# First gate/up phase: w_down sums and block combinations on GpSimd, with their stores on GpSimd's queue

## The chip, the cores and the metric

The kernel runs on one core of a Trainium2 chip. A core has TensorE (matrix products into PSUM, PE in the profile), VectorE (DVE), ScalarE (ACT), GpSimd (POOL) and SyncE (SP), which only issues transfers. Each engine works through its own instructions strictly in order; semaphores hold an instruction back until what it needs is there. A transfer (DMA) is issued by an instruction in the queue of SP, ACT or GpSimd and then runs by itself. The metric is the device time of one execution in microseconds, as the median of several runs.

## The reference

The kernel computes one decoder layer over 2048 tokens of width 1024 in float32. What is behind the change is its feed-forward part:

```python
hn = rms_norm(h, ffn_pre_g)
ff = (jax.nn.silu(hn @ w_gate) * (hn @ w_up)) @ w_down      # 1024 -> 2816 -> 1024
h = h + rms_norm(ff, ffn_post_g)
```

Before it come an input projection, sliding-window attention, a causal convolution of width 31 over 512 channels (its 31 multiplications and additions per position are called taps) and an output projection.

## The kernel before, in words

Every product of two float32 matrices is made of three passes of a reduced format (`F32R`): each operand is split into a high part (ACT copies it, line 782 for the weights of this stage) and a low part (the rest, a subtraction on DVE or GpSimd, line 786 or, where DVE's helper records it, line 85), and high-high, high-low and low-high are added up in PSUM (line 108 is the matmul of all stages).

The tokens are taken in four tiles of 512. The feed-forward part works on two tiles at once, and there are two rounds: tiles 0 and 1 (names end in F for the gate/up phase and G for the down projection; in the code `ws[0]` is 0), then tiles 2 and 3 (`ws[0]` is 2). Inside a round, the two halves of the tokens and the two halves of the features make 2 x 2 blocks, and a scheme of seven block products instead of eight is used. For gate and up (`stage_p1`), the weight blocks A11 to A22 of a pair of 128-column groups give sums S1 to S4 (on DVE, `chl@F`), the activations' sums T1 to T4 are made once. A pair of column groups is worked for the gate and then for up; each takes five steps of 12 matmuls where two of the seven products were made earlier (`stage_pre`; their partial sums are kept in DRAM as `keeps` and loaded back into `gb`), and seven where not (the last of the 11 pairs).

The outputs of a pair are four blocks: the gate's goes through Silu on ACT into a tile `fa` (line 1038), the up product is multiplied onto it on DVE. `fa` has four buffers, so ACT can write a pair's outputs only when the stores of the pair before have read the same buffers. The down projection (`stage_p2`) is again the scheme of seven products; its operands are the four blocks and their sums, and the seven kinds are stored in DRAM as `mids`. Line 1045 stores a block as it is (two of a pair, and three in the last pair; in the other ten the third was stored by `stage_pre` and is loaded back by line 1014); then four combinations are made in place (lines 1050 and 1053), each overwriting a block, and stored (lines 1051 and 1054). A combination that overwrites a block that is being stored waits until that store has landed. In both rounds these later stores are put off by two steps (`defer`) and bound to the matmul of that time (`tied`), and they are issued by SP. In round one the combinations run on DVE (`vtt`), in round two on GpSimd (`ptt`).

The same scheme needs sums of w_down's blocks. `stage_tsums` makes them once, beside the first gate/up phase: for each of 11 pairs four blocks are loaded (line 1072, into `wx`, one buffer of two halves, and two of the three buffers of `fc`), four subtractions are made on DVE (`wx@G`, `fc@G`), and each result is stored as `td` (line 1078) by SP. A pair's buffers can be loaded again when its stores have landed.

Beside the main line run lanes, generators that are advanced by a fixed rate per step: the convolution's taps on DVE (`fc@C`), the sums of w_down, the output projection of later tiles. All this only gives the order in which instructions are emitted. A scheduler then fixes the order on each engine, by its own estimate of when each can run, and assigns buffers; the chip runs that order.

SP issues nearly all loads: raw weights (lines 956 and 958), the kept partial sums (line 988), w_down (1072). A store in its queue whose operand isn't ready holds up the loads behind it.

Of the kernel before, what the change touches and what calls it, by code (L numbers as in the profile page):

```python
# [18 lines left out]
ALU = mybir.AluOpType  # L19
# [18 lines left out]
def layer_kernel(ctx, tc, x, xT, cols, rows, sinks, relb, onehot, w_in, w_pw, w_out, w_gate, w_up, w_down, out):  # L38
    nc = tc.nc
# [15 lines left out]
    def t_(tag, shape, dt=F32):  # L55
        return sb.tile(list(shape), dt, tag=tag, name=nm(tag), bufs=BUFS[tag])

    def f4(tag, shape=(P, D)):
        return t_(tag, shape)

    def f2(tag, shape=(P, T)):
        return t_(tag, shape)

    def hl(tag):
        return t_(tag, (P, 2, T), F32R)
# [17 lines left out]
    def dve(op):  # L83
        def emit(*args, **kw):
            r = op(*args, **kw)  # L85
            if not paced[0]:
                pace["main"] = r.ins
            elif pace["main"] is not None and pace["main"] is not pace["tied"]:
                tc.add_manual_dep(
                    r.ins,  # L90
                    pace["main"].name,
                    mybir.DependencyInfo(mybir.DependencyClass.NoSync, mybir.DependencyReason.DATA),
                    reason="conv taps keep pace with the projections",
                )
                pace["tied"] = pace["main"]
            return r

        return emit

    stt = dve(nc.vector.scalar_tensor_tensor)  # L100
    vtt = dve(nc.vector.tensor_tensor)
    vts = dve(nc.vector.tensor_scalar)
    ptt = nc.gpsimd.tensor_tensor
# [9 lines left out]
    def tied(r):  # L113
        if lead_pe[0] is not None and lead_pe[0] is not r:
            after_first(lead_pe[0], r)
        return r
# [3 lines left out]
    def defer(n, emit):  # L120
        later.append([n, emit])

    def run_later():
        for item in later:
            item[0] -= 1
        while later and later[0][0] <= 0:
            later.pop(0)[1]()
# [52 lines left out]
    def after_first(first, r):  # L180
        tc.add_manual_dep(
            r.ins,
            first.ins.name,
            mybir.DependencyInfo(mybir.DependencyClass.NoSync, mybir.DependencyReason.DATA),
            reason="order",
        )
# [594 lines left out]
    def split_f(x, w):  # L781
        act(w[:, 0], x, AF.Copy)  # L782
        return w

    def lo(x, w, on_pool):
        (ptt if on_pool else vtt)(w[:, 1], x, w[:, 0].bitcast(F32), ALU.subtract)
# [155 lines left out]
    def stage_p1(ws, ops, mid, keep):  # L942
        PRE = PRES[ws[0]]
        L = f"F{ws[0]}"
        raws = {}
        todo = []
        for m in range(len(MATS)):
            st = [1, 2, 4, 5, 6] if m < PRE else list(range(7))
            todo += [(m, j, i, len(st)) for j, i in enumerate(st)]

        def loads(m):
            if m < len(MATS):
                lab[0] = L
                src, pr = MATS[m]
                r0 = t_("raw", (P, 2, T))
                nc.sync.dma_start(r0, src[2 * pr].rearrange("p (a b) -> p a b", a=2))
                r1 = t_("chl", (P, 2, T))
                nc.sync.dma_start(r1, src[2 * pr + 1].rearrange("p (a b) -> p a b", a=2))
                raws[m] = dict(A11=r0[:, 0], A12=r0[:, 1], A21=r1[:, 0], A22=r1[:, 1])

        def sums(m):
            if m < len(MATS):
                lab[0] = L
                r = raws[m]
                s12 = t_("chl", (P, 2, T))
                r["S1"], r["S2"] = s12[:, 0], s12[:, 1]
                vtt(r["S1"], r["A21"], r["A22"], ALU.add)
                vtt(r["S2"], r["S1"], r["A11"], ALU.subtract)
                s34 = t_("chl", (P, 2, T))
                r["S3"], r["S4"] = s34[:, 0], s34[:, 1]  # L970
                vtt(r["S3"], r["A11"], r["A21"], ALU.subtract)
                vtt(r["S4"], r["A12"], r["S2"], ALU.subtract)

        wops = {}
        kept = {}

        def split(q):
            if q < len(todo):
                m, j, i, n = todo[q]
                lab[0] = L  # L980
                wops[q] = split_f(raws[m][STEPS[i][1]], hl("w"))
                lo(raws[m][STEPS[i][1]], wops[q], ws[0] and i in POOL_LO)

        def fetch(m):
            if m < PRE:
                lab[0] = L
                kept[m] = f2("gb")
                nc.sync.dma_start(kept[m], keep[m])

        loads(0)  # L990
        sums(0)
        for q in range(AHEAD):
            split(q)
        loads(1)
        fetch(0)
        sg = {}
        for q, (m, j, i, nst) in enumerate(todo):
            pre = m < PRE
            gate = MATS[m][0] is w_gate
            pr = MATS[m][1]  # L1000
            run_later()
            split(q + AHEAD)
            lab[0] = L
            which, an, bn = STEPS[i]
            if len(ops.get(bn, ())) < 4:
                lh.until(f"S{ws[0]}")
                lab[0] = L
            if j == 0:
                bk = {}
                if not gate:  # L1010
                    blocks = {}
                    if pre:
                        blocks[3] = f2("fa")
                        nc.sync.dma_start(blocks[3], mid[0, pr])
                if pre:
                    bk["B"] = mm()
                    act(bk["B"], kept.pop(m), AF.Copy)
            first = which not in bk
            if first:
                bk[which] = mm()  # L1020
            o = bk[which]
            product(o, wops.pop(q), ops[bn], first)
            if i == 0:
                bk["B"] = mm()
                act(bk["B"], o, AF.Copy)
            elif i == 1:
                y5 = f2("gb")
                act(y5, o, AF.Copy)
            elif i == 2:
                x2 = f2("at")  # L1030
                act(x2, o, AF.Copy)  # L1031
            else:
                v = {4: y5, 5: x2}.get(i, o)
                if v is not o:
                    vtt(v, v, o, ALU.add)
                if gate:
                    s = f2("fa")
                    act(s, v, AF.Silu)
                    sg[i] = s
                else:  # L1040
                    s = sg.pop(i)
                    vtt(s, s, v, ALU.mult)
                    blocks[i] = s
                    if i in (3, 4, 6):
                        nc.sync.dma_start(mid[{3: 0, 4: 4, 6: 1}[i], pr], s)
                    if i == 5:
                        a11, a22, a21 = blocks[3], blocks[4], s
                        for to, o_, p_, op, q_ in ((5, a22, a21, ALU.add, a22), (3, a21, a11, ALU.subtract, a21),
                                                   (2, a11, a22, ALU.subtract, a11)):
                            (ptt if ws[0] else vtt)(o_, p_, q_, op)  # L1050
                            defer(2, lambda a=mid[to, pr], o_=o_: tied(nc.sync.dma_start(a, o_)))
                    if i == 6:
                        (ptt if ws[0] else vtt)(s, s, blocks[3], ALU.subtract)
                        defer(2, lambda a=mid[6, pr], s=s: tied(nc.sync.dma_start(a, s)))
            if j == nst - 4:
                sums(m + 1)
            if j == nst - 2:
                fetch(m + 1)
            if j == nst - 1:
                loads(m + 2)  # L1060
            yield 2.76
        run_later()
        run_later()

    def stage_tsums(td):
        L = "G0"
        for pr in range(NF // 2):
            lab[0] = L
            wx = f4("wx", (P, 2, T))
            b = [wx[:, 0], wx[:, 1], f2("fc"), f2("fc")]  # L1070
            for i, (f, n) in enumerate(((0, 0), (0, 1), (1, 0), (1, 1))):
                tied(nc.sync.dma_start(b[i], w_down[2 * pr + f, :, n * T : (n + 1) * T]))
            yield 3
            b11, b12, b21, b22 = b
            for to, o, p_, q_ in ((0, b11, b12, b11), (2, b12, b22, b12), (1, b22, b22, b11), (3, b21, b21, b22)):
                lab[0] = L
                vtt(o, p_, q_, ALU.subtract)
                nc.sync.dma_start(td[to, pr], o)
                yield 1

    def finish(L, gb, jobs, pool=True):
# [317 lines left out]
    td = dr.tile([4, NF // 2, P, T], F32, name="td")  # L1399
    keeps = [dr.tile([PRES[2 * i], P, T], F32, name=f"keeps{i}") for i in range(2)]  # L1400
    ws, ops = (0, 1), {}
# [12 lines left out]
    ws, ops = (2, 3), {}  # L1414
# [76 lines left out]
```

## Time and profile before

| | |
|---|---|
| runs | 2039.29, 2031.3, 2038.7 us; median 2038.7 |
| the profiled execution | 2035.91 us |
| its span | 2034.2 us |
| TensorE busy | 1960.4 us, 96% of the span |
| VectorE busy | 1504.4 us, 74% |
| ScalarE busy | 986.4 us, 48% |
| GpSimd busy | 402.8 us, 20% |

The page lists busy time by engine, then the span in 40 equal slices with the busy share in tenths. A row of the groups of instructions has line, engine, operation, output<-inputs, shapes and count, then busy microseconds and mean nanoseconds, then the idle time of the engine just before and what ended it. A row of the timeline has start, duration, engine, line, operation and count; in brackets the idle time before it and the instruction that ended it. A row by stretch has the stretch, its length, and for PE, PEld (weight loads), DVE, ACT and POOL the busy time and the number of instructions, then the granted clock of TensorE, the DMA share and GB/s. SPq is SP's queue of transfers; a row of transfers ends in KB and in the median time from issue to landing.

### The profile page before, as it was taken

What the parts mean: (1) busy time and instruction counts of PE and PEld (TensorE: products, weight loads), DVE (VectorE), ACT (ScalarE), POOL (GpSimd) and SP (SyncE); (2) the same over time, 40 slices, a digit from 0 to 9 for tenths busy, and PEclk for the clock granted to TensorE, in tenths of its full rate; (3) what the DMA queues carried; (4) which work ended last, traced back from release to release, by engine and by line L of the source; (5) the groups of instructions that cost most, each with busy time, mean ns of one, the idle gap of its engine ahead of it and who ended that gap; (6) DMA issues with size and microseconds to landing.
All of it is one profiled execution on the core that took longest, in us unless ns stands there. A gap on an engine that the chain in (4) does not pass through costs nothing. (4 is left out here: it accounts for less than half of the span.)

```text
span 2034.2 us, 27180 instructions
## 1 busy us (share of the span) xinstructions
PE 1960.4 (96%) x8826; PEld 1566.7 (77%) x8826; DVE 1504.4 (74%) x2649; ACT 986.4 (48%) x1938; POOL 402.8 (20%) x462
## 2 busy tenths in 40 slices
PE   8999999998989999999989999999999999999998
PEld 6877767776667778788878878877788888888886
DVE  5999886994795889888649985577566665545557
ACT  5455445456546633333346457556643333345443
POOL 6011224433111300000001012115423233220000
PEclk9999999999999999999999999999999999999999
DMA  8787645578558876777376778579954443266654
GB/s 309 257 300 232 204 135 186 182 233 275 174 179 313 293 240 225 263 247 251 139 264 211 234 261 283 193 278 305 335 182 159 149 174 114 95 232 227 193 186 166
DMA packets 234110, 451.44 MB, mean 222 GB/s; under 512 B 23496, under 2 KB 49264, under 8 KB 233968
## 3 DMA queue, kind: packets, MB, share of 16 engines
q1 hardware_dynamic: 211184, 411.96, 60.9%
q10 hardware_dynamic: 20544, 30.42, 4.1%
q0 software_dynamic: 2240, 7.34, 0.9%
q8 instruction: 69, 1.13, 0.2%
q14 instruction: 73, 0.60, 0.1%
HBM read 330.60 MB, written 119.02 MB: 221 GB/s over the span
## 5 line engine op out<-in xcount | busy, mean ns | idle before, releaser
L85 DVE SCALAR_TENSOR_TENSOR fc@C<-glu@C,colt,fc@C 128x512 f32<-128x512 f32 x480 | 373.3, 791 | 3.0
L108 PE MATMUL mm@F<-hl@H,w@F 128*128 128x512 f32 x1056 | 252.4, 390 | 2.7 <-ACT mm@F L909 2.5
L108 PE MATMUL mm@G<-hl@G,hl@G 128*128 128x512 f32 x924 | 228.8, 397 | 7.0 <-DVE x@G L85 4.6
L108 PEld LDWEIGHTS mm@F<-hl@H,w@F 128*128 128x128 f32 x1056 | 197.8, 188 | 44.6 <-ACT mm@F L909 3.6
L108 PEld LDWEIGHTS mm@G<-hl@G,hl@G 128*128 128x128 f32 x924 | 173.7, 190 | 46.2 <-ACT hl@G L782 6.3
L108 PE MATMUL mm@A<-hl@A,w@A 128*128 128x512 f32 x840 | 206.6, 397 | 2.4 <-ACT hl@A L318 1.4
L782 ACT ACTIVATE w@F<-chl@F 128x512 fp32r<-128x512 f32 x220 | 135.4, 625 | 141.6 <-PE mm@F L108 134.8
L108 PE MATMUL mm@G<-w@G,hl@G 128*128 128x512 f32 x876 | 199.5, 389 | 0.0
L108 PEld LDWEIGHTS mm@G<-w@G,hl@G 128*128 128x128 f32 x876 | 164.5, 188 | 34.1
L108 PEld LDWEIGHTS mm@A<-hl@A,w@A 128*128 128x128 f32 x840 | 156.0, 189 | 38.0 <-DVE hl@A L85 2.3
L85 DVE TENSOR_TENSOR w@F<-chl@F,w@F 128x512 fp32r<-128x512 f32 x198 | 144.6, 732 | 35.8 <-ACT w@F L782 35.4
L108 PE MATMUL mm@F<-ql@H,w@F 128*128 128x512 f32 x528 | 128.5, 391 | 4.8 <-ACT w@F L782 3.1
L108 PE MATMUL mm@F<-mid@H,w@F 128*128 128x512 f32 x528 | 130.6, 392 | 2.3 <-ACT mm@F L909 2.2
L108 PE MATMUL mm@F<-p@H,w@F 128*128 128x512 f32 x528 | 131.5, 395 | 0.3 <-ACT at@F L1031 0.3
L108 PE MATMUL mm@F<-x@H,w@F 128*128 128x512 f32 x528 | 126.9, 394 | 2.3 <-ACT fa@F L931 2.3
L108 PEld LDWEIGHTS mm@F<-ql@H,w@F 128*128 128x128 f32 x528 | 98.9, 188 | 27.0 <-ACT w@F L782 3.8
L108 PEld LDWEIGHTS mm@F<-x@H,w@F 128*128 128x128 f32 x528 | 100.0, 190 | 23.9 <-ACT fa@F L931 2.8
L108 PEld LDWEIGHTS mm@F<-mid@H,w@F 128*128 128x128 f32 x528 | 98.9, 189 | 25.1 <-ACT mm@F L909 3.7
L108 PEld LDWEIGHTS mm@F<-p@H,w@F 128*128 128x128 f32 x528 | 100.7, 191 | 22.1 <-ACT at@F L1031 0.9
L133 ACT ACTIVATE w@A<-raw@A 128x512 fp32r<-128x512 f32 x110 | 67.6, 627 | 94.0 <-PE mm@A L108 54.8
L108 PE MATMUL mm@W<-w@W,hl@W 128*128 128x512 f32 x384 | 100.8, 406 | 9.2 <-ACT hl@W L704 5.9
L108 PE MATMUL tr@W<-w@W,ql@W 128*128 128x512 f32 x384 | 98.7, 396 | 5.6 <-ACT mid@W L675 4.6
(302 smaller groups left out, 3385.7 us busy)
## 6 DMA issues: line engine op xcount, KB each, us to landing
mids<-fa@F SPq DMA_DIRECT2D x154, 256.0 KB, 2.6
raw@A<-w_in SPq DMA_DIRECT2D x55, 512.0 KB, 4.5
w@A<-lo_in SPq DMA_DIRECT2D x84, 256.0 KB, 3.4
fc@G<-mids SPq DMA_DIRECT2D x77, 256.0 KB, 3.4
fa@G<-mids SPq DMA_DIRECT2D x75, 256.0 KB, 4.5
gb@F<-keeps SPq DMA_DIRECT2D x72, 256.0 KB, 4.3
raw@W<-w_out SPq DMA_DIRECT2D x32, 512.0 KB, 5.5
w@W<-lo_out SPq DMA_DIRECT2D x48, 256.0 KB, 3.7
```

The lines of the kernel that those rows point to most:

```text
L85: r = op(*args, **kw)
L108: r = nc.tensor.matmul(*args, **kw)
L133: act(w[:, 0], raw, AF.Copy)
L782: act(w[:, 0], x, AF.Copy)
```

## The change

In round one (`ws[0]` is 0) the four combinations of each pair go from DVE to GpSimd, the six stores of each pair (seven in the last) from SP's queue to GpSimd's, and the delay of two steps and the binding to a matmul fall away for the four later ones. The four subtractions of each w_down pair go from DVE to GpSimd and their stores from SP to GpSimd. Round two stays as it is. In all 88 operations and 111 stores change their place; no operation is added or left out.

```diff
                     if i in (3, 4, 6):
-                        nc.sync.dma_start(mid[{3: 0, 4: 4, 6: 1}[i], pr], s)
+                        (nc.sync if ws[0] else nc.gpsimd).dma_start(mid[{3: 0, 4: 4, 6: 1}[i], pr], s)
                     if i == 5:
                         a11, a22, a21 = blocks[3], blocks[4], s
                         for to, o_, p_, op, q_ in ((5, a22, a21, ALU.add, a22), (3, a21, a11, ALU.subtract, a21),
                                                    (2, a11, a22, ALU.subtract, a11)):
-                            (ptt if ws[0] else vtt)(o_, p_, q_, op)
-                            defer(2, lambda a=mid[to, pr], o_=o_: tied(nc.sync.dma_start(a, o_)))
+                            ptt(o_, p_, q_, op)
+                            if ws[0]:
+                                defer(2, lambda a=mid[to, pr], o_=o_: tied(nc.sync.dma_start(a, o_)))
+                            else:
+                                nc.gpsimd.dma_start(mid[to, pr], o_)
                     if i == 6:
-                        (ptt if ws[0] else vtt)(s, s, blocks[3], ALU.subtract)
-                        defer(2, lambda a=mid[6, pr], s=s: tied(nc.sync.dma_start(a, s)))
+                        ptt(s, s, blocks[3], ALU.subtract)
+                        if ws[0]:
+                            defer(2, lambda a=mid[6, pr], s=s: tied(nc.sync.dma_start(a, s)))
+                        else:
+                            nc.gpsimd.dma_start(mid[6, pr], s)
...
             for to, o, p_, q_ in ((0, b11, b12, b11), (2, b12, b22, b12), (1, b22, b22, b11), (3, b21, b21, b22)):
                 lab[0] = L
-                vtt(o, p_, q_, ALU.subtract)
-                nc.sync.dma_start(td[to, pr], o)
+                ptt(o, p_, q_, ALU.subtract)
+                nc.gpsimd.dma_start(td[to, pr], o)
                 yield 1
```

## The prediction

> **What bounds the kernel now.** I read the page first, then the busy time by stretch of the stage that changes, then the gaps of TensorE in it, then what ended each gap.
>
> ```profile
> span 2034.2 us, 27180 instructions
> PE 1960.4 (96%) x8826; PEld 1566.7 (77%) x8826; DVE 1504.4 (74%) x2649; ACT 986.4 (48%) x1938; POOL 402.8 (20%) x462
> ...
> DVE  5999886994795889888649985577566665545557
> ...
> POOL 6011224433111300000001012115423233220000
> ...
> DMA  8787645578558876777376778579954443266654
> ```
>
> TensorE is busy 96% of the span: only about 74 us are its gaps, and an edit elsewhere can win no more than the gaps of its own stage. POOL does nothing in slices 15 to 21, and in the first five of these DVE stands at 8 and 9 tenths: that is the first gate/up phase. The next fence is the busy time by stretch: the stretch of the w_down sums, the rest of the phase, the change to the down projection, and for comparison the second gate/up phase, in which the block combinations already run on GpSimd and SP issues their stores.
>
> ```profile
> 716.00:945.00 229.00, 221.31 (x951) 180.95 (x950) 200.08 (x323) 84.23 (x151) 0.00 (x0) 0.98 0.74 248
> 945.00:1029.50 84.50, 84.50 (x375) 69.56 (x374) 56.88 (x91) 33.51 (x60) 0.00 (x0) 1.00 0.52 175
> 1029.50:1060.00 30.50, 24.84 (x105) 19.22 (x104) 16.96 (x28) 16.07 (x31) 0.00 (x0) 0.94 0.83 270
> 1500.00:1820.00 320.00, 320.00 (x1414) 265.05 (x1413) 193.48 (x251) 123.72 (x219) 94.11 (x66) 1.00 0.44 153
> ```
>
> TensorE idles 229.00 - 221.31 = 7.7 us beside the w_down sums, nothing after them, and 30.50 - 24.84 = 5.7 us at the change of stages. 13.4 us is all that this edit can win directly. The three large gaps, and what stood before each in DVE's, ACT's and SP's timelines:
>
> ```profile
> 728.71 2.90 PE L108 MATMUL mm@F<-yt@H,w@F 128*128 128x512 f32 x6 [3.60 <-DVE gb@F L85]
> 727.36 0.69 DVE L85 TENSOR_TENSOR wx@G<-wx@G 128x512 f32<-128x512 f32 x1 [2.28 <-DMA wx@G<-w_down]
> 727.97 0.68 DVE L85 TENSOR_TENSOR gb@F<-gb@F,mm@F 128x512 f32<-128x512 f32 x1
> 835.45 1.22 PE L108 MATMUL mm@F<-ql@H,w@F 128*128 128x512 f32 x2 [3.06 <-ACT w@F L782]
> 834.25 0.60 ACT L1017 ACTIVATE mm@F<-gb@F 128x512 f32<-128x512 f32 x1 [8.80 <-DMA gb@F<-keeps]
> 824.05 3.00 SPq L1078 DMA_DIRECT2D td<-wx@G  x2
> 828.89 0.42 SPq L988 DMA_DIRECT2D gb@F<-keeps  x1
> 1049.36 6.00 PE L108 MATMUL tr@W<-w@W,ql@W 128*128 128x512 f32 x18 [4.65 <-ACT mid@W L675]
> 1048.19 0.63 ACT L704 ACTIVATE ql@W<-at@W 128x512 fp32r<-128x512 f32 x1 [5.11 <-DMA at@W<-mixT]
> 1041.40 0.40 SPq L1051 DMA_DIRECT2D mids<-fa@F  x1
> 1041.90 0.39 SPq L702 DMA_DIRECT2D at@W<-mixT  x1
> ```
>
> The first gap: DVE stood 2.28 us before a w_down sum whose load had not landed, and the addition that frees a bank stood behind it. The second: ACT waited 8.80 us for a kept partial sum, whose load went out at 828.89 behind w_down stores that SP held until DVE was done. The third is the same at the end: a load for the output projection behind a store of the last block.
>
> **The change part by part.**
>
> *Off DVE.* 44 w_down sums (four kinds, 11 each) and 44 combinations (40 in the phase proper, 4 at its end):
>
> ```profile
> L85 DVE TENSOR_TENSOR wx@G<-wx@G 128x512 f32<-128x512 f32 x11 | 7.6, 690 | 7.5 <-DMA wx@G<-w_down 6.7 <-DMA fc@G<-w_down 0.8
> L85 DVE TENSOR_TENSOR fc@G<-fc@G,wx@G 128x512 f32<-128x512 f32 x11 | 7.5, 683 | 0.0
> L85 DVE TENSOR_TENSOR fa@F<-fa@F,fa@F 128x512 f32<-128x512 f32 x40 | 27.4, 685 | 4.9 <-DMA mids<-fa@F 4.8
> L1050 POOL TENSOR_TENSOR fa@F<-fa@F,fa@F 128x512 f32<-128x512 f32 x33 | 46.2, 1399 | 59.0 <-DMA mids<-fa@F 34.8 <-issue 8.2 <-DVE chl@F L85 8.0
> L1053 POOL TENSOR_TENSOR fa@F<-fa@F,fa@F 128x512 f32<-128x512 f32 x11 | 16.6, 1510 | 10.9 <-DVE chl@F L85 6.0 <-DMA mids<-fa@F 3.6 <-DVE w@F L85 1.2
> L1078 SPq DMA_DIRECT2D td<-wx@G x22: 319/323/431, 717.0 to 939.6; - x22
> L1051 SPq DMA_DIRECT2D mids<-fa@F x30: 319/320/998, 750.1 to 1000.9; - x30
> 323.52 0.57 POOL L137 DMA_DIRECT2D lo_out<-w@W  x1 [0.30 <-POOL w@W L135]
> L137 POOL DMA_DIRECT2D lo_out<-w@W x16: 539/557/587, 315.9 to 411.2; - x16
> mids<-fa@F SPq DMA_DIRECT2D x154, 256.0 KB, 2.6
> lo_out<-w@W POOLq DMA_DIRECT2D x16, 256.0 KB, 4.8
> lo_in<-w@A POOLq DMA_DIRECT2D x12, 256.0 KB, 5.6
> wx@G<-w_down SPq DMA_DIRECT2D x22, 256.0 KB, 4.8
> ```
>
> The stores of three combinations per block pair run from 750.1 to 1000.9 for ten pairs, so a pair lasts some 27 us and 8 pairs lie before 945. In that stretch 44 + 32 = 76 operations leave DVE; its queue goes forward 0.61 us with each (727.36 to 727.97): 46 us of its 200. This alone is worth what waits for DVE, the first gap above, 3.6 us at most; what then comes last is ACT and the transfers.
>
> *Off SP.* 44 + 67 stores (six a pair, seven in the last). Its loads no longer stand behind operands that are not ready: this can remove the second gap (3.1 us) and the third (4.7 us). SP still has to hold each w_down load until the tile's earlier store has landed, and the loads of raw weights and kept sums stand behind it as before.
>
> *Onto GpSimd.* One operation costs 1.40 to 1.51 us there. I take 1.51, since DVE is denser here (200.08 of 229) than in the second phase (193.48 of 320) where these rows come from. A store costs the queue 0.557 us, and 0.30 us pass between an operation and its own store. In the 229 us: 76 x 1.51 = 114.8, 44 + 48 = 92 stores x 0.557 = 51.2, 76 x 0.30 = 22.8; together 188.8 us, where there was nothing. The queue has room, but it is in order, and two waits are added to it. They hang on how long a store of GpSimd takes to land: 5.6 us at the start of the kernel (DMA line of the page: 8 tenths), 4.8 between 316 and 411 us (5 or 6 tenths); here the share is 0.74, so I take 5.2.
>
> First wait: a block that is stored as it is and then overwritten by a combination. The store must land first: 5.2 us less its own issue and one sum that stands between, 3.1 us. Second wait: in the changed program's order, in 6 of the 10 passages from one w_down group to the next, only a sum, its store and one more store stand between the last store of a group and the second sum of the next, some 3.5 us with that last store's own issue; but this sum's operand needs that store landed and a new load landed, 5.2 + 4.8 = 10 us. So 6 x 6.5 = 39 us. In four of these six the first wait falls into the second; four of the eight pairs are left, 12 us. Sum 188.8 + 39 + 12 = 240 us against 229: 11 us more. The lateness reaches TensorE in two ways: the four output tiles of the multiplications come free when GpSimd's stores have landed and ACT, in order, waits for one with bank seeds and weight splits behind it; and SP waits for w_down stores with weight and partial-sum loads behind it. How much of the first kind TensorE bears today, by ACT's timeline:
>
> ```profile
> 756.55 0.63 ACT L1038 ACTIVATE fa@F<-gb@F 128x512 f32<-128x512 f32 x1 [3.39 <-DMA mids<-fa@F]
> 813.67 0.64 ACT L1038 ACTIVATE fa@F<-gb@F 128x512 f32<-128x512 f32 x1 [3.45 <-DVE fa@F L85]
> 813.06 1.65 PE L108 MATMUL mm@F<-yt@H,w@F 128*128 128x512 f32 x6 [0.32 <-DVE gb@F L85]
> ```
>
> ACT stood 3.4 us twice, and TensorE lost nothing the first time and 0.32 us the second; I let lateness past some 3 us count in full. The stores' old delay of two steps falls away (ten steps make a pair, so 5 us); GpSimd's own order, as counted, uses that up.
>
> Ends: at 1.399 per operation 8 us less; with stores landing in 4.8 or 5.6 us, 10 x 0.4 = 4 us less or more; if the second wait comes in all ten passages, 26 us more. Below nothing: 13.4 us, all gaps gone. Of the 7.7 us of gaps I let half remain, 4 us, because two in-order queues that are both nearly full don't run evenly. At the change of stages 4.7 us go, but the last tiles come free nearly 3 us later (5.2 against 2.6 us landing), and the down projection's loads wait for these: -2.
>
> Sum: +11 + 4 - 2 = +13 us on 2035.91 us (span 2034.2 and 1.7 around it). The median shown, 2038.7, lies 2.8 above this execution; I forecast on the median: 2038.7 + 13 = about 2052 us.
>
> DVE does not get its 46 us for nothing. Two of its instructions with both inputs in SBUF, while GpSimd works (from the two timelines):
>
> ```profile
> 683.88 1.67 POOL L786 TENSOR_TENSOR p@H<-chl@H,p@H 128x512 fp32r<-128x512 f32 x1 [0.25 <-ACT p@H L855]
> 684.32 1.78 DVE L85 TENSOR_TENSOR w@F<-raw@F,w@F 128x512 fp32r<-128x512 f32 x1
> 685.50 1.75 POOL L786 TENSOR_TENSOR mid@H<-chl@H,mid@H 128x512 fp32r<-128x512 f32 x1
> 686.02 1.78 DVE L85 TENSOR_TENSOR ql@H<-chl@H,ql@H 128x512 fp32r<-128x512 f32 x1
> ```
>
> Each takes 1.78 us where its kind takes 0.68, and ends about 0.5 us after GpSimd's: 1.10 us lost per GpSimd operation, 76 x 1.10 = 84 us at most. DVE would then need 200 - 46 + 84 = 238 us of 229; it needs less where its next instruction reads PSUM or isn't ready. So I count DVE as neither relieved nor the bound, and take no gain beyond the gaps. Nor can later stages win: in the changed program's order DVE has as many convolution taps behind it at the start of the down projection as before (421), so its saved time takes no work out of that stage.
>
> **The rivals.**
>
> *DVE becomes the bound.* Each GpSimd operation shuts DVE out for its whole 1.51 us: 76 x 1.51 = 115 us, DVE needs 200 - 46 + 115 = 269 us of 229: +40, less 2 at the end: 2077. For it: the four rows above. Against: the second phase, where TensorE loses nothing (320.00 of 320) beside 66 GpSimd operations. It decides where DVE nearly always has a two-input instruction ready. [...] That DVE waits to GpSimd's end the rows above agree with; what it costs hangs on how often DVE is ready then, and no row of this phase shows it.
>
> *Faster: GpSimd keeps up.* All 13.4 us of gaps go: 2025. It decides where GpSimd's stores land as soon as SP's, in 2.6 us: the second wait is then 2.6 + 4.8 - 3.5 = 3.9 us, six times 23, the first is nothing, and 188.8 + 23 = 212 us fit beside TensorE's 221.3. For it: the second phase again, and SP's queue, which is left with loads alone. Against: 4.8 and 5.6 us to landing. [...]
>
> *Hidden.* GpSimd is late now and then, but TensorE has slack for it, some gaps go and some come: -6 to +8, around 2039. For it: the two waits of ACT for an output tile quoted above, which cost TensorE nothing or 0.3 us. It decides if GpSimd is never more than some 3 us late.
>
> **How the numbers follow.** Forecast (2049 to 2066) 0.40, DVE bound or every passage late (to 2084) 0.15, hidden 0.28, faster 0.17. 0.5% is 10.2 us, about what a measurement of this kernel can tell from no change. Slower by more: 0.40 + 0.15 = 0.55; within: 0.28; faster: 0.17, of which half lies below 2028. Range 2028 to 2080; that of the likeliest case 2049 to 2066.
>
> **What would show it.** In the changed profile: POOL busy some 115 us in operations alone, about 1.5 us each, in the stretch of the w_down sums; that stretch longer than 229 us; ACT's multiplication outputs and SP's w_down loads waiting for GpSimd's stores, 4.8 us to landing; DVE's two-input instructions stretched beyond 0.69 us; no gap behind DVE's w_down sum. The forecast is wrong if TensorE stays without gaps there, or if GpSimd's stores land in under 3 us.

## The result and the profile after

The changed kernel takes 2086.81 us (median of 5), the kernel before 2037.66 us (median of 5): ratio 1.0242, 95% interval 1.0219 to 1.0266, so 49 us slower, outside the range of 2028 to 2080. The profiled execution of the changed kernel took 2092.36 us; it is the slowest of the five, so the two profiled spans differ by 56 us where the medians differ by 49.

The page of the changed kernel, the lines that answer to the first fence of the prediction:

```profile
span 2090.6 us, 27204 instructions
PE 1984.2 (95%) x8826; PEld 1581.0 (76%) x8826; DVE 1554.9 (74%) x2561; ACT 987.5 (47%) x1938; POOL 581.6 (28%) x661
...
DVE  5999886993985898988857996477666666546557
...
POOL 6012123441122345554431102105423333220000
```

The span grew by 56.4 us. TensorE executes the same 8826 matmuls, but is busy 1984.2 - 1960.4 = 23.8 us longer with them; the other 32.6 us are new idle time. DVE executes 88 instructions fewer and is busy 50.5 us longer. The busy time by stretch of the changed kernel (columns as in the prediction) shows where:

```profile
716.00:1002.00 286.00, 252.83 (x1010) 202.36 (x1008) 253.91 (x264) 88.97 (x160) 147.96 (x165) 0.92 0.60 207
1002.00:1080.00 78.00, 75.72 (x329) 62.52 (x330) 54.84 (x69) 29.45 (x52) 21.14 (x25) 0.98 0.50 172
1554.00:1874.00 320.00, 320.00 (x1414) 264.99 (x1413) 194.82 (x253) 125.64 (x224) 95.07 (x67) 1.00 0.44 150
```

The stretch of the w_down sums, 229 us before, lasts about 286. TensorE stands still for 286.00 - 252.83 = 33.2 us of it, where it was 7.7, and its granted clock is 0.92, where it was 0.98. GpSimd is busy 148 us of the 286, so it is not full. The second gate/up phase (last line) is as it was. Who keeps TensorE, SP and GpSimd waiting is in the waits of the changed kernel from 700 to 1090 us (sum in us, how many times, the longest):

```profile
PE mm@F L108 <- DVE gb@F L85: 21.2, 7, 4.9
PE mm@F L108 <- DVE w@F L85: 6.2, 3, 3.3
PE mm@F L108 <- DVE fa@F L85: 3.2, 1, 3.2
PE mm@F L108 <- DVE at@F L85: 3.0, 1, 3.0
...
SPq L956 <- DVE chl@F L85: 155.7, 20, 19.9
SPq L958 <- DVE w@F L85: 75.1, 20, 12.6
...
POOL wx@G L1083 <- DMA wx@G<-w_down: 84.0, 8, 27.9
POOL fa@F L1050 <- DMA mids<-fa@F: 17.3, 5, 5.0
```

33.6 us of TensorE's waits end with DVE. In the same view of the kernel before, from 700 to 1040 us, the first row has 3.9 us and SP's two rows read:

```profile
PE mm@F L108 <- DVE gb@F L85: 3.9, 2, 3.6
...
SPq L956 <- DVE chl@F L85: 22.8, 16, 4.0
...
SPq L958 <- DVE w@F L85: 21.1, 19, 3.4
```

DVE became late, although 88 operations were taken off it. The groups of DVE's instructions from 716 to 1030 us, first before, then after:

```profile
L85 DVE TENSOR_TENSOR w@F<-chl@F,w@F 128x512 fp32r<-128x512 f32 x105 | 71.5, 684 | 5.4 <-ACT w@F L782 5.3
L85 DVE SCALAR_TENSOR_TENSOR fc@C<-glu@C,colt,fc@C 128x512 f32<-128x512 f32 x63 | 46.7, 744 | 0.0
...
L85 DVE TENSOR_TENSOR chl@F<-raw@F,chl@F 128x512 f32<-128x512 f32 x40 | 26.2, 684 | 0.2
L85 DVE TENSOR_TENSOR gb@F<-gb@F,mm@F 128x512 f32<-128x512 f32 x21 | 14.3, 682 | 11.7 <-PE mm@F L108 11.7
```

```profile
L85 DVE TENSOR_TENSOR w@F<-chl@F,w@F 128x512 fp32r<-128x512 f32 x94 | 103.0, 1101 | 1.2 <-ACT w@F L782 1.1
L85 DVE SCALAR_TENSOR_TENSOR fc@C<-glu@C,colt,fc@C 128x512 f32<-128x512 f32 x56 | 60.5, 1082 | 0.1
L85 DVE TENSOR_TENSOR chl@F<-raw@F,chl@F 128x512 f32<-128x512 f32 x38 | 50.1, 1356 | 0.4
L85 DVE TENSOR_TENSOR chl@F<-chl@F,raw@F 128x512 f32<-128x512 f32 x19 | 20.8, 1094 | 0.3
...
L85 DVE TENSOR_TENSOR gb@F<-gb@F,mm@F 128x512 f32<-128x512 f32 x18 | 12.2, 679 | 6.7 <-PE mm@F L108 6.7
```

The first four groups of the second fence, whose instructions have two inputs in SBUF (the memory of the core in which all tiles lie that are not in PSUM), take 1.08 to 1.36 us in place of 0.68 to 0.74; the one with an input in PSUM (gb@F) is unchanged at 0.68. The excess of the four stretched groups is 94 x 0.417 + 56 x 0.338 + (50.1 - 38 x 0.684) + 19 x 0.410 = 90 us. Here is one gap of TensorE, followed back, and a time of its slow pace, by the timelines of GpSimd, DVE and TensorE in the changed kernel:

```profile
756.49 1.77 POOL L1083 TENSOR_TENSOR wx@G<-fc@G,wx@G 128x512 f32<-128x512 f32 x1 [2.02 <-DMA fc@G<-w_down]
758.55 0.56 POOL L1084 DMA_DIRECT2D td<-wx@G  x1 [0.30 <-POOL wx@G L1083]
759.13 1.29 POOL L1083 TENSOR_TENSOR fc@G<-fc@G,wx@G 128x512 f32<-128x512 f32 x1
760.36 1.27 POOL L1050 TENSOR_TENSOR fa@F<-fa@F,fa@F 128x512 f32<-128x512 f32 x1
...
757.03 1.77 DVE L85 SCALAR_TENSOR_TENSOR fc@C<-glu@C,colt,fc@C 128x512 f32<-128x512 f32 x1
758.73 3.47 DVE L85 TENSOR_TENSOR chl@F<-chl@F,raw@F 128x512 f32<-128x512 f32 x1
762.12 0.68 DVE L85 TENSOR_TENSOR fa@F<-fa@F,mm@F 128x512 f32<-128x512 f32 x1
...
749.88 2.93 PE L108 MATMUL mm@F<-yt@H,w@F 128*128 128x512 f32 x6 [3.52 <-DVE gb@F L85]
752.61 2.76 PE L108 MATMUL mm@F<-mid@H,w@F 128*128 128x512 f32 x6
755.17 1.16 PE L108 MATMUL mm@F<-ql@H,w@F 128*128 128x512 f32 x3
...
762.85 2.93 PE L108 MATMUL mm@F<-mid@H,w@F 128*128 128x512 f32 x6 [3.21 <-DVE fa@F L85]
```

A tap that took 1.77 us ended 0.54 after GpSimd's sum (758.80 against 758.26). A weight sum (chl@F) began at 758.73, while GpSimd issued a store and before its next operations began; it was not let through until both of those (759.13 and 760.36) had ended, and took 3.47 us. Behind it stood the multiplication that empties a bank, one of the parts of PSUM that matmuls fill (762.12), and TensorE stood 3.21 us until that was done. TensorE's rows show the price after a gap as well: six matmuls take 2.93 us, where behind the short gap that the prediction quotes (813.06) they took 1.65. After the gap at 749.88 three rows have 2.93 + 2.76 + 1.16 = 6.85 us for 15 matmuls; at 1.65 for six that would be 4.13, so 2.7 us more are lost behind a gap of 3.52. The granted clock from 749.8 to 756.2 us is 0.53; from 756.2 to 758.9 it is 1.00 again.

### The profile page after: what moved, and what is told of

Its sections match the earlier page's. It is cut to its first block, busy times and chain, and to the rows that moved or that the text cites. A ratio compares the mean times of both kernels' runs of the same rounds, so it can differ in the third digit from the quotient of the medians.

```text
span 2090.6 us, 27204 instructions
## 1 busy us (share of the span) xinstructions
PE 1984.2 (95%) x8826; PEld 1581.0 (76%) x8826; DVE 1554.9 (74%) x2561; ACT 987.5 (47%) x1938; POOL 581.6 (28%) x661
## 5 line engine op out<-in xcount | busy, mean ns | idle before, releaser
L85 DVE SCALAR_TENSOR_TENSOR fc@C<-glu@C,colt,fc@C 128x512 f32<-128x512 f32 x480 | 392.3, 831 | 3.0
L85 DVE TENSOR_TENSOR w@F<-chl@F,w@F 128x512 fp32r<-128x512 f32 x198 | 185.4, 941 | 36.3 <-ACT w@F L782 35.9
L108 PE MATMUL mm@F<-mid@H,w@F 128*128 128x512 f32 x528 | 142.3, 416 | 14.5 <-DVE w@F L85 3.3
L108 PEld LDWEIGHTS mm@F<-mid@H,w@F 128*128 128x128 f32 x528 | 104.9, 201 | 41.8 <-ACT mm@F L909 5.2
L108 PEld LDWEIGHTS mm@F<-x@H,w@F 128*128 128x128 f32 x528 | 100.0, 190 | 23.8 <-ACT fa@F L931 2.8
L499 POOL TENSOR_SCALAR_AFFINE_SELECT p@B<-p@B 128x512 f32<-128x512 f32 x62 | 57.3, 933 | 211.6 <-ACT p@B L497 210.3
L1050 POOL TENSOR_TENSOR fa@F<-fa@F,fa@F 128x512 f32<-128x512 f32 x66 | 90.4, 1370 | 87.7 <-DMA mids<-fa@F 53.3
```

The lines of the kernel that those rows point to most:

```text
L108: r = nc.tensor.matmul(*args, **kw)
L499: nc.gpsimd.affine_select(out=pg[:, kb].rearrange("p (i q) -> p i q", q=P), in_=pg[:, 1].rearrange("p (i q) -> p i q", q=P), compare_op=AL ...
L1050: ptt(o_, p_, q_, op)
```

## The experiments

Three theories were put against each other. The port theory: a GpSimd operation that reads SBUF holds back DVE's instructions with two SBUF inputs (it is named after the access to SBUF that the two would share; the runs show who is held back, not the port itself). The issue theory: GpSimd's issue of a store does so as well. The queue theory, that of the forecast: results and buffers are late because GpSimd's queue is in order and waits for stores.

### Operations alone, stores alone

The 88 operations alone (stores on SP, put off as before):

```diff
-                            (ptt if ws[0] else vtt)(o_, p_, q_, op)
+                            ptt(o_, p_, q_, op)
...
-                vtt(o, p_, q_, ALU.subtract)
+                ptt(o, p_, q_, ALU.subtract)
                 nc.sync.dma_start(td[to, pr], o)
```

> Only the 88 operations go to GpSimd; the 111 stores stay with SP, put off and bound as before. Port theory (a GpSimd operation that reads SBUF holds back every DVE instruction with two SBUF inputs): the loss stays whole, 2075 to 2095 us, DVE's w@F sums at 0.95 us or more where before has 0.68. Issue theory (the 0.55 us in which GpSimd issues a store hold DVE back as well): 92 x 0.55 = 51 us of the 155 us that GpSimd works in the stretch are gone, so a third of the 49 us, 2065 to 2075. Queue theory (GpSimd's order of operations and stores, and what waits for its stores): 2030 to 2050, DVE's sums still short.

The 111 stores alone (from the changed kernel, `vtt` again in place of `ptt`):

```diff
-                            ptt(o_, p_, q_, op)
+                            (ptt if ws[0] else vtt)(o_, p_, q_, op)
...
-                ptt(o, p_, q_, ALU.subtract)
+                vtt(o, p_, q_, ALU.subtract)
                 nc.gpsimd.dma_start(td[to, pr], o)
```

> Only the 111 stores go to GpSimd's queue, the 88 operations stay on DVE. Port theory: GpSimd reads no operand, so DVE's w@F sums stay at 0.68 to 0.72 us; SP no longer holds loads behind stores that are not ready, so the gaps of TensorE at 835 and 1049 us may go: 2028 to 2040 us. Issue theory: 111 x 0.55 = 61 us in which DVE is held back, a third of the loss, 2050 to 2065, sums at 0.8 us or more. Queue theory: between, 2035 to 2050.

Operations alone: 2059.65 us, ratio 1.0101 (1.0084 to 1.0117). Stores alone: 2038.33 us, ratio 1.0000 (0.9986 to 1.0014). The groups of DVE's instructions (716 to 1030 us), operations alone and then stores alone:

```profile
L85 DVE TENSOR_TENSOR w@F<-chl@F,w@F 128x512 fp32r<-128x512 f32 x102 | 94.0, 923 | 10.9 <-ACT w@F L782 10.9
```

```profile
L85 DVE TENSOR_TENSOR w@F<-chl@F,w@F 128x512 fp32r<-128x512 f32 x104 | 70.8, 684 | 6.1 <-ACT w@F L782 6.1
```

The issue theory falls: 111 issues on GpSimd leave DVE's durations as they were. The time of the run with stores alone lies in the ranges of both other theories. Every theory missed the run with operations alone: the loss is 21 us, not 49, nor is it nothing. So operations and stores together cost 28 us more than the sum of each alone.

### Half of the change each

The w_down sums with their stores, as an edit of the kernel before:

```diff
-                vtt(o, p_, q_, ALU.subtract)
-                nc.sync.dma_start(td[to, pr], o)
+                ptt(o, p_, q_, ALU.subtract)
+                nc.gpsimd.dma_start(td[to, pr], o)
```

> Only the 44 sums of w_down and their stores go to GpSimd; the block combinations stay on DVE and SP. Port theory: 44 of the 76 operations that stand beside the dense DVE, so 44/76 of 49 us = 28 us: 2058 to 2070. Queue theory: 2035 to 2050, since GpSimd's queue is little loaded and its stores land in 2.6 us.

And the block combinations with the blocks' stores, as the same lines undone in the changed kernel:

```diff
-                ptt(o, p_, q_, ALU.subtract)
-                nc.gpsimd.dma_start(td[to, pr], o)
+                vtt(o, p_, q_, ALU.subtract)
+                nc.sync.dma_start(td[to, pr], o)
```

> Only the 44 block combinations and the 67 stores of the blocks go to GpSimd; the sums of w_down stay on DVE and SP. Port theory by count: 32 of the 76 operations of the dense stretch, 32/76 of 49 us = 21 us, so 2053 to 2066. If an operation that stands behind a store's issue in GpSimd's queue gets the port ahead of DVE's instruction, more, since here issue and operation alternate: up to 2075. Queue theory: 2036 to 2048.

Sums alone: 2066.13 us, ratio 1.0134 (1.0118 to 1.0150), 27 us. Combinations alone: 2068.62 us, ratio 1.0145 (1.0119 to 1.0170), 30 us. Both are outside the queue's ranges. The first is inside the port's; the second is above what the count of operations gives and inside the wider range for operations that stand behind a store's issue. 44 operations with stores from the same queue cost more than 88 operations with stores on SP.

### Operations that read nothing

```diff
+    def zero3(o):
+        for _ in range(3):
+            nc.gpsimd.memset(o, 0.0)
...
-                            ptt(o_, p_, q_, op)
+                            if ws[0]:
+                                ptt(o_, p_, q_, op)
+                            else:
+                                zero3(o_)
```

(likewise for the other moved operations of the phase; `memset` fills a tile, here with zeros)

> The changed kernel, but each moved operation of the first gate/up phase is replaced by three fills of its output with zeros on GpSimd (the sums and combinations are left out; the stores and their queue stay). A fill writes SBUF and reads nothing. Port theory, read side alone: DVE's w@F sums at 0.68 to 0.75 us and no loss, 2025 to 2042 us. Port theory, write side too: DVE's sums stretched as in the changed kernel, 2070 or more. Queue theory: GpSimd's queue is as full as in the changed kernel or fuller, so 2075 to 2100. Issue theory: the issues remain, 2050 to 2065.

2034.36 us, ratio 0.9974 (0.9964 to 0.9983). The page's engine line, the stretch of the sums and DVE's weight sums (line numbers of the kernels with inserted lines are shifted by a few):

```profile
PE 1957.8 (97%) x8826; PEld 1563.5 (77%) x8826; DVE 1454.7 (72%) x2561; ACT 987.1 (49%) x1938; POOL 589.0 (29%) x837
```

```profile
716.00:945.00 229.00, 224.90 (x984) 185.33 (x983) 164.01 (x259) 87.60 (x156) 151.17 (x305) 0.99 0.75 254
```

```profile
L85 DVE TENSOR_TENSOR w@F<-chl@F,w@F 128x512 fp32r<-128x512 f32 x103 | 70.5, 686 | 14.4 <-ACT w@F L787 14.3
```

GpSimd is as busy as in the changed kernel (589.0 against 581.6 us) and issues the same stores, but DVE's durations are those of before and TensorE's gaps in the stretch fall to 4.1 us. The whole loss is gone, and with it the queue theory as its cause: 52 us between two kernels whose GpSimd is equally busy. Nor was it the time that stores take to land: in the run with fills the 67 stores of the blocks landed in 4.5 us, longer than in the changed kernel (2.7) and near the forecast's 5.2 (the w_down stores in 2.8 and 3.5), and nothing was lost. It is the reading, not the writing: beside fills, which only write, DVE's w@F sums took 686 ns, beside the operations, which read as well, 1101.

Fills don't wait for the second operand of the sum they stand for. So in a further run each set of fills was followed by the operation itself on 64 of 512 columns, with its own operands:

```diff
             zero3(o_)
+            ptt(o_[:, 0:64], p_[:, 0:64], q_[:, 0:64], op)
```

> The run with fills, and behind the fills of each moved operation the operation itself on 64 of its 512 columns, with its own operands: so every wait for operands and buffers that the changed kernel has is there, GpSimd's queue holds more instructions than the changed kernel's, and only the time in which GpSimd reads SBUF is small (the rest of each sum is left out). Port theory: about 1/8 to 1/4 of the 93 us by which DVE is stretched, few of it on the path; 2032 to 2048 us, DVE's w@F sums at 0.69 to 0.80 us. Queue theory (waits for operands, for stores, order of the queue): 2075 to 2100.

2048.85 us, ratio 1.0047 (1.0029 to 1.0065): 0.85 us above the port's range and far below the queue's; DVE's w@F sums take 711 ns. That is 10 us over the kernel before and 14.5 over the run with fills alone. Little of it is DVE: 27 ns on some 200 instructions is 5 us, spread over the phase. The waits of ACT (716 to 1030 us) point to the rest:

```profile
ACT fa@F L1043 <- DMA mids<-fa@F: 27.7, 11, 4.9
```

Before, the same wait was 9.2 us in 3 times. So the forecast's queue effect exists, at some 2 us of GpSimd for each operation (three fills of 0.54 and the rest), and is worth 14.5 us at most there. In the changed kernel, with 1.3 to 1.4 us for each, this wait is 1.1 us, once.

### Why operations and stores together cost more

```diff
-                        (nc.sync if ws[0] else nc.gpsimd).dma_start(mid[{3: 0, 4: 4, 6: 1}[i], pr], s)
+                        nc.sync.dma_start(mid[{3: 0, 4: 4, 6: 1}[i], pr], s)
...
-                nc.gpsimd.dma_start(td[to, pr], o)
+                nc.sync.dma_start(td[to, pr], o)
```

> The changed kernel with all 111 stores of the phase issued by SP, at once, not put off by two steps. It stands between the run with operations alone (2059.65 us, stores on SP, put off) and the changed kernel (2086.81). If the extra 27 us come from operations that stand behind a store's issue in GpSimd's own queue and so get the port first: 2055 to 2066, DVE's w@F sums near 0.92 us. If they come from the stores' missing delay: 2078 to 2090, sums near 1.10 us.

2059.08 us, ratio 1.0087 (1.0062 to 1.0112), w@F sums 940 ns: as with the stores put off, so the delay is worth nothing, and the 28 us come from stores and operations sharing a queue. DVE's groups say the same: summed over its instructions with two SBUF inputs from 716 to 1030 us, the time beyond 0.685 us (taps: 0.744) is 57 us with operations alone, 58 with the stores on SP at once and 92 in the changed kernel. The timelines of DVE and GpSimd from 716 to 1030 us tell how. I took DVE's instructions without an operand in PSUM that stand alone in their row, and sorted them by what GpSimd did when they began (the last two columns are two runs with fills, told below); the numbers are how many, and their mean time beyond 0.685 us (taps: 0.74):

| begins | operations alone | stores alone | changed | one fill | six fills |
|---|---|---|---|---|---|
| while an operation runs | 53, 0.76 | - | 26, 1.00 | 28, 0.68 | 37, 0.69 |
| while a store is issued, an operation begins within 0.9 us | - | - | 22, 1.97 | 40, 1.23 | 1, 0.0 |
| while a store is issued, none begins | - | 64, 0.00 | 12, 0.00 | 13, 0.00 | 40, 0.00 |
| while a fill runs, an operation begins within 0.9 us | - | - | - | 6, 0.37 | 31, 0.00 |
| while GpSimd is idle, an operation begins within 0.9 us | 23, 0.00 | - | 16, 0.07 | 13, 0.00 | 2, 0.0 |

Where DVE begins first and GpSimd is idle, GpSimd's operation waits: with operations alone it takes 1.48 to 1.6 us in its groups' means, against 1.3 to 1.41 in the changed kernel. Where DVE begins during the issue of a store with an operation close behind, DVE loses, though it began first, and waits for that whole operation. In the changed kernel most operations stand directly behind a store, and those that beat DVE in the second row began 0.01 to 0.03 us after the end of an issue. Two runs put fills of a scratch tile between them:

```diff
+    def gstore(to, tile_):
+        r = nc.gpsimd.dma_start(to, tile_)
+        spacer[0] = nc.gpsimd.memset(scr, 0.0)
+        after_first(r, spacer[0])
+
+    def gop(*args):
+        r = ptt(*args)
+        if spacer[0] is not None:
+            after_first(spacer[0], r)
```

(`gstore` stands for the phase's stores, `gop` for its moved operations; `after_first(a, b)` puts b behind a in its engine's order. The second run repeats the fill six times, with 64 columns.)

> The changed kernel, with a fill of an 8-column scratch tile behind each of GpSimd's stores of the phase, so that no moved operation stands directly behind a store in GpSimd's queue (in the changed kernel 63 of 73 in the stretch of the w_down sums do). In the runs so far a two-input instruction of DVE that begins during a store's issue is stretched only if such an operation follows, and one that begins during a fill is not. If standing directly behind the issue is what lets the operation take the port first: the loss falls towards that of the two runs with stores on SP (2059 us), 2055 to 2072, DVE's w@F sums at 0.90 to 1.00 us. If any queued operation takes it, or the loss comes from the stores' place itself: 2080 to 2092, sums near 1.10 us.

> As the run with one small fill behind each store of GpSimd, but six fills of 64 columns, so that a moved operation begins 0.5 us or more after the end of the issue. If an operation can take the port ahead of DVE only while the issue has just ended: DVE's w@F sums at 0.90 to 1.00 us and 2055 to 2070 us, in spite of a fuller queue. If an operation that stands anywhere behind a store takes it: sums at 1.10 us, 2074 to 2092.

One fill of 8 columns (0.12 us): 2078.21 us, ratio 1.0193 (1.0164 to 1.0223), w@F sums 1114 ns. DVE is still beaten, so the place in the queue directly behind the store is not what counts. But the fill put little time between the two: of the 40 instructions in the second row, 31 lost 1.36 to 1.63 us, and there the operation began 0.06 or 0.07 us after the end of the issue. Nine lost nothing: in seven of them the operation began 0.61 us or more after DVE's instruction, when that was about done, and in the two others it began 0.10 and 0.24 us after the issue. Six fills: 2089.97 us, ratio 1.0254 (1.0229 to 1.0279), where the first expectation had 2055 to 2070. It missed because the fills took 1.21 us, not 0.6 as I had reckoned:

```profile
719.72 0.59 POOL L107 DMA_DIRECT2D td<-wx@G  x1 [0.30 <-POOL wx@G L114]
720.32 1.21 POOL L109 MEMSET scr<- 128x64 f32 x6
721.50 1.69 POOL L114 TENSOR_TENSOR wx@G<-fc@G,wx@G 128x512 f32<-128x512 f32 x1
```

111 stores with 1.21 us behind each are 134 us more in GpSimd's queue, 231 us busy of the 314 from 716 to 1030, and now TensorE waits where the queue theory has it wait: 35.8 us in 8 times for partial sums that ACT copies into its banks, and ACT itself waits 19.2 us for GpSimd's combinations and 16.8 for their stores. But DVE is freed: no instruction of 31 that began in a fill ahead of an operation was stretched (last column), and the w@F sums fell to 810 ns, below even the first expectation. So an operation well behind the issue does not go ahead of an instruction of DVE that began in the fills. Whether what counts is the short time since the issue, or that DVE's instruction began during the issue, these runs hardly separate: with six fills the operation began only when an instruction begun during the issue was done, and the one-fill run has two cases. Why GpSimd goes first, the trace does not show.

### Is it DVE's lack of time?

The 63 taps of the phase left out, in the kernel before and in the changed one:

```diff
-                stt(y, g[:, j : j + T], dwh[:, c, j : j + 1], y, ALU.mult, ALU.add)
+                if not skip[0]:
+                    stt(y, g[:, j : j + T], dwh[:, c, j : j + 1], y, ALU.mult, ALU.add)
```

> The kernel before, with the 63 taps of the convolution that fall into this phase left out (63 x 0.744 = 47 us of DVE's work; the convolution of the third tile is incomplete). It is the base of the next run: by every theory TensorE loses its gaps behind DVE at most, 2028 to 2040 us.

> The changed kernel with the taps of this phase left out in the same way. Port theory, by which the loss is DVE's lack of time: DVE has 47 us less to do and can bear the 93 us by which its instructions are stretched; at most 12 us over the run before this one, 2030 to 2050. Queue theory (results late behind GpSimd's queue and stores): the loss stays, 35 us or more over the run before this one, 2065 to 2085.

2038.32 us (ratio 0.9995, 0.9978 to 1.0011) and 2061.14 us (ratio 1.0103, 1.0080 to 1.0125): 23 us between them. Neither expectation held: the loss is halved, not gone. With 47 us less to do, DVE waits more for its weights instead, and TensorE's gaps are mostly shorter:

```profile
L85 DVE TENSOR_TENSOR w@F<-chl@F,w@F 128x512 fp32r<-128x512 f32 x103 | 106.5, 1037 | 9.2 <-ACT w@F L785 9.1
...
L85 DVE TENSOR_TENSOR chl@F<-chl@F 128x512 f32<-128x512 f32 x19 | 17.0, 896 | 45.1 <-DMA chl@F<-w_up 23.2 <-DMA chl@F<-w_gate 21.8
```

So about half of the loss went with DVE's sum of work. The other half is left although DVE, stretched by 85 us in all, then stands idle for 65 of the 314 us from 716 to 1030. What suggests itself is the single stretched instruction in front of a bank's release, as in the chain above, and the loop by which a late weight sum holds SP's next weight load (the waits on L956), which DVE then waits for; no run separates these two, and this stays open.

### What the stores alone are worth

Only the 44 w_down stores to GpSimd's queue, and the same with the sums emitted later behind their loads:

```diff
-                nc.sync.dma_start(td[to, pr], o)
+                nc.gpsimd.dma_start(td[to, pr], o)
```

> The kernel before with only the 44 stores of the w_down sums issued by GpSimd; all operations stay on DVE. By the trace of before, SP holds a load of a kept partial sum behind two such stores, and TensorE then stands 3.06 us at 835 us. Port theory: DVE's durations unchanged, that gap shrinks or goes: 2033 to 2039 us. Issue theory: slower by the share of 44 x 0.55 = 24 us that reaches DVE, 2045 to 2055.

```diff
-            yield 3
+            yield 6
             b11, b12, b21, b22 = b
...
-    RT = 0.3
+    RT = 0.43
```

> The same, and the sums of each w_down pair are emitted twice as long behind their loads (6 instead of 3 units, at a rate of 0.43 instead of 0.30, so that a pair takes as long as before). It aims at the largest gap, 3.60 us at 729 us behind DVE's wait for a w_down load. If DVE's wait for those loads (12 us in all) is what the gaps hang on: 2030 to 2037 us. If other loads take its place: 2036 to 2041.

2034.86 us, ratio 0.9984 (0.9971 to 0.9998), inside the port's range, and 2036.53 us, ratio 0.9987 (0.9975 to 0.9999), which lies in both ranges. In the first the gap at 835 us shrank from 3.06 to 0.59; in the second the gap at 729 us shrank from 3.60 to 0.59, and others took its place. They gain 3 and 2 us at the median, less than the 0.5% that I took as telling; of the versions that do all of the computation these two alone came out ahead of the kernel before, and only just.

## Why the prediction was wrong

The forecast had the kernel slower, by 13 us and because GpSimd would be late; it became slower by 49 us and because DVE was held back. That the direction was right is, in the main, luck.

**Off DVE: the step that failed.** It stood there as "I count DVE as neither relieved nor the bound". The four rows quoted for it were the right ones, and the 84 us that it called the most were reached in full: the stretched groups lost 90 us in 716 to 1030 us, 1.1 us for each of GpSimd's 80 operations there, even though only part of DVE's instructions have two SBUF inputs. An operation moved gives DVE 0.61 us and takes 1.1, so DVE became the bound. I had set 238 us of need against a stretch of 229 and then counted it as nothing.

**Onto GpSimd: its price was too high.** Sums and combinations took 1.30 to 1.41 us, not 1.51, and the landing of stores, on which +11 us hung, was not 5.2 us. The DMA rows of the changed kernel:

```profile
mids<-fa@F POOLq DMA_DIRECT2D x67, 256.0 KB, 2.7
...
td<-wx@G POOLq DMA_DIRECT2D x22, 256.0 KB, 2.5
td<-fc@G POOLq DMA_DIRECT2D x22, 256.0 KB, 2.6
```

The 4.8 and 5.6 us came from other stages with other transfers beside them; SP's stores of the same tiles would have been the nearer rows: 2.6 us for the blocks in the row quoted, which holds both rounds, 2.9 in this phase alone. Landing is no fixed figure even in this phase (4.5 us in the run with fills). The first wait came (17.3 us in 5 times, 12 forecast), but GpSimd had room for it. In place of the second GpSimd waited 84 us for w_down loads, 27.9 of them before the first sum; SP waited once, for 0.9 us, for a w_down store ahead of such a load. GpSimd waited for SP, which waited for DVE, not the other way round.

**Off SP: right in size and worth nothing.** With the stores alone moved, the gap at 835 us went from 3.06 to 1.18 and the one at the change of stages from 4.65 to 3.35, and new gaps of 0.6 to 2.4 us took it back (ratio 1.0000). In the changed kernel the gap at the change of stages is 5.27 us; the -2 did not come.

**The clock: not in the sum at all.** A term is missing for what follows a gap. Busy time of TensorE by the pages, and gaps of 2 us or more from 700 to 1110 us: before 1960.4 and 3, changed kernel 1984.2 and 11, sums alone 1973.8 and 7, combinations alone 1972.5 and 6, operations alone 1965.4 and 6, stores at once on SP 1963.0 and 6, changed kernel without taps 1964.0 and 6. That is some 1 to 4 us on top of each gap more, and rough, since runs with 3 gaps have 1957.8 to 1962.9; in the changed kernel it is 24 of the 56 us of the two profiled spans. My own third fence had it: after the first gap six matmuls took 2.90 us.

**The rivals.** "DVE becomes the bound" had the right mechanism and came to 2077, 10 us short. Its 40 us stand against 32.6 us of new idle time of TensorE, and the 23.8 us that TensorE was busy longer it did not have; that it came near is in part luck. It shared 15 chances in 100 with another case, for I held against it the second phase with its 320.00 of 320. That comparison held only for a DVE that is busy 193 of 320 us, and with the stores on SP. "GpSimd keeps up" had its condition fulfilled to the figure, stores landing in 2.6 us, and the kernel is still 49 us slower: the condition was not the deciding one. Of the signs named, the longer stretch and DVE's stretched instructions came, and POOL's operations came to 102 us in that stretch at 1.36 each, not 115 at 1.5; ACT's outputs and SP's w_down loads waiting for GpSimd's stores did not (1.1 and 0.9 us). The forecast named as its own refutation that the stores land in under 3 us; they did, and the time was missed on the other side.

## What to carry to other kernels

Before moving an operation from VectorE to GpSimd to relieve VectorE, count what it will take from VectorE as well: beside a VectorE that was 87% busy, mostly with instructions that have two inputs in SBUF, an operation of 1.3 to 1.4 us on GpSimd gave back 0.61 us and took 1.1. If it must be moved, keep GpSimd's stores away from it in the queue, since that cost 28 of the 49 us here, and a store alone cost nothing. And price a stall of TensorE of 2 us or more at its length and, on average in these runs, another 1 to 4 us.

## What the runs showed of the hardware that I had not expected

In these runs a GpSimd operation that began right behind a store's issue (0.01 to 0.03 us after its end in the changed kernel, 0.06 or 0.07 with one small fill between) went ahead of a DVE instruction with two SBUF inputs that had begun during that issue and was not done. In the changed kernel the 22 instructions of that row of the table lost 1.97 us each on average, while none of 64 was stretched where GpSimd had stores and no operations. Where GpSimd was idle it was the other way round: of DVE's instructions that began up to 0.9 us before an operation, 23 lost 0.00 us each with operations alone, and 16 lost 0.07 us in the changed kernel.

TensorE's slow pace followed some gaps of about 2 us and not others. With the block combinations alone on GpSimd one gap of 2.21 us and one of 1.89 were followed by it, while with one fill behind each store a gap of 2.33 us was not:

```profile
949.78 2.22 PE L108 MATMUL mm@F<-yt@H,w@F 128*128 128x512 f32 x6 [2.21 <-DVE gb@F L85]
881.82 2.47 PE L108 MATMUL mm@F<-mid@H,w@F 128*128 128x512 f32 x6 [1.89 <-DVE fa@F L85]
...
769.92 1.65 PE L122 MATMUL mm@F<-yt@H,w@F 128*128 128x512 f32 x6 [2.33 <-DVE gb@F L85]
```

The granted clock in the 2.3 to 3.2 us from these matmuls on is 0.71, 0.59 and 1.00. With the sums alone a gap of 2.17 us was followed by six matmuls in 2.61, and gaps of 1.83 and 1.96 us in the runs with operations or sums alone by six in 1.65 and 1.66, the full pace there; in the changed kernel without taps a gap of 2.53 us was not followed by a slow stretch. So the length of the gap alone does not decide.
